# A hybrid decoder block on one core: gate tables, rank sums, and the order of two stages

## The chip, the cores and the metric

The kernel runs on one core of one Trainium2 chip. The metric is the time of one execution on the device in microseconds (us); lower is better. Engines are named as in the profile: PE is TensorE (PEld its weight loads), DVE is VectorE, ACT is ScalarE, POOL is GpSimd, and SP is SyncE, which only issues transfers.

## The reference

One decoder block over 1024 tokens of width 1024. Two mixers run in parallel on one projected input, an RWKV-7 recurrence and an attention that keeps 256 keys per query by an indexer. Sigmoid gates merge them, an output projection and a layer norm follow. Then comes a PEER mixer, the part that matters here. For each token and each of 8 heads a query is scored against two sets of 128 sub-keys; the 16 best of each set give 256 sums, the 16 best sums pick 16 experts out of 128 x 128 with softmax gates:

```
s1, i1 = top_k(s[:, :, 0], 16);  s2, i2 = top_k(s[:, :, 1], 16)
top_s, pos = top_k(s1[..., :, None] + s2[..., None, :], 16)      # flattened to 256
experts = i1[pos // 16] * 128 + i2[pos % 16];  gates = softmax(top_s)
act = gelu(h @ u[experts]) * gates;  y = sum(act * v[experts])
```

A second residual and layer norm close the block. All data are float32.

## The kernel before

The sequence is handled in two halves of 512 tokens (H = 0, 1) up to the end of the first norm. A planner lays out each engine's instructions ahead of the run, by its own model of times and by the order in which the program issues them; on the chip each engine keeps the order it was given. Several program parts are generators, and `next(side)` issues one step of another part in between.

**Merge** (`merge`, L1006). For a half, eight projections of the recurrence's output (first loop, L1016), eight of the merged rows (second loop, L1034; L1044 makes the residual sums), the norm, then eight query projections for the PEER mixer (L1092). In the second half the side work is the retrieval of token tiles 1 and 2 (a tile is 128 tokens). A step is issued in each turn of the first two loops.

**Retrieval** (`retrieve`, L1117). Six steps a tile: four of scores (a load of queries on SyncE's queue, eight matmuls against the keys, VectorE's top 16 with positions), one that merges candidates, one that turns positions into expert numbers. That last one needs sums of 16 ranks: `weighted` (L1187) multiplies 64 x 16 values in bf16 and adds them in four halvings (L1192 to L1196). It runs six times a tile.

**Two ways for the experts.** Tiles 0 to 2 gather their experts' rows one by one (`peer_gather`, L1344): GpSimd issues an indirect transfer of 128 rows (L1371), VectorE multiplies and adds (L1375 for u, L1379 for v). These gathers are spread over all of the second half of the kernel. Tiles 3 to 7 (640 tokens, `DN`) compute all 16384 experts densely and weigh them by a table of gates.

**Gate tables** (`gate_table`, L1241). For each token of tiles 3 to 7, TensorE multiplies a one-hot matrix of the second keys (128 slots x 128 keys) with one of the first keys scaled by the gates. In blocks of 8 tokens, VectorE compares the second keys (L1247, 128x1024), makes six of the eight first-key matrices (L1252) with the gate in the same instruction, and ScalarE the other two (L1254, L1255). Four tokens share a PSUM bank `tp`; a token's 128 results stand next to each other, and ScalarE's copy into `st` (L1262) reorders them, so that a key's tokens are neighbours. `st` goes to DRAM as `gtD`. Retrieval of tiles 3 to 7 and their tables run together; meanwhile TensorE computes the dots of 69 of the 128 key rows ahead of time (`dots_u`, L1630), six matmuls in each of eight steps k, from `h2T` (two halves, high and low part of the split, loaded on GpSimd's queue, L1603).

**Dense part** (L1635). 16 groups of 8 key rows. `dense_u` makes a row's activations: dots on TensorE and the gelu (L1313), or for a row ahead a load and the gelu (L1310); then the gates (L1315, from a buffer `gt` that holds four rows' gates, two buffers) and the split into two halves (L1317). `dense_v` multiplies the group before with eight column blocks of v, a block in eight steps, one per row; L1331 adds into `yacc`. Two blocks follow each of the first four rows. From the second group on, the first row that is not ahead is moved to the front (`lead`). Rows and blocks take turns in three pairs of PSUM banks (`pair`).

Of the kernel before, what the change touches and what calls it, by code (L numbers as in the profile page):

```python
# [8 lines left out]
F32 = mybir.dt.float32  # L9
# [22 lines left out]
ONE_HOT = 6  # L32
# [14 lines left out]
QS = 1  # L47
# [156 lines left out]
def body(tc, a, out, dbg=None, ntiles=8, mark=lambda s: None):  # L204
# [138 lines left out]
    ident, iota, iotan = (base.tile([128, 128], F32, name=n) for n in ("ident", "iota", "iotan"))  # L343
# [13 lines left out]
    def constants():  # L357
# [15 lines left out]
        V.tensor_scalar(iotan, iota, -1.0, None, op0=OP.mult)  # L373
# [632 lines left out]
    def merge(H, y, bz, mp, side, ties):  # L1006
# [9 lines left out]
        for d in range(8):  # L1016
# [14 lines left out]
            if H or d % QS == QS - 1:  # L1031
                next(side, None)
        vt = mp.tile([128, 8, 512], F32, name="vt")
        for d in range(8):  # L1034
# [12 lines left out]
            next(side, None)  # L1047
# [44 lines left out]
        for h in range(8):  # L1092
            w = split_w(a["wq"][h], 1024)
            pt = pacc()
            proj(pt, w, (h2T[:, 0], h2T[:, 1]), 8)
            qt = stg.tile([128, 512], F32, name="zs")
            copy(qt, pt)
            nc.sync.dma_start(qTD[H][:, h, :], qt)
        for d in range(8 if c0 < 512 else 0):
# [17 lines left out]
    def retrieve(i, keysT, tp_, then):  # L1117
# [69 lines left out]
        def weighted(ge, wt, dst):  # L1187
# [4 lines left out]
            V.tensor_tensor(pr[:, :, 0:8], pr[:, :, 0:8], pr[:, :, 8:16], op=OP.add)  # L1192
            s4 = tp_.tile([128, 64, 8], F32, name="wx")
            V.tensor_tensor(s4[:, :, 0:4], pr[:, :, 0:4], pr[:, :, 4:8], op=OP.add)
            V.tensor_tensor(s4[:, :, 0:2], s4[:, :, 0:2], s4[:, :, 2:4], op=OP.add)
            V.tensor_tensor(dst, s4[:, :, 0], s4[:, :, 1], op=OP.add)  # L1196
# [3 lines left out]
        start = tp_.tile([128, 128], BF, name="start")  # L1200
# [30 lines left out]
    def by_slot(found, dst):  # L1231
# [3 lines left out]
        for n, src in enumerate((i1, i2, gates)):  # L1235
            nc.tensor.transpose(tp[:, n * 128:(n + 1) * 128], src, ident)
        copy(dst[:, 0, :], tp[:, 0:128], scale=-1.0)
        copy(dst[:, 1:3, :].rearrange("p a b -> p (a b)"), tp[:, 128:384])


    def gate_table(i, slots, sl, du, st):  # L1241
        ng = sl.tile([128, 128], F32, name="ng")
        V.tensor_scalar(ng, slots[:, 2, :], -1.0, None, op0=OP.mult)
        for b in range(max(0, TD - i * 128) // 8, 16):
            s_ = st[:, b // 4 % 2]
            oh = du.tile([128, 16, 128], F32, name="gt", bufs=2)
            V.tensor_tensor(oh[:, 0:8], iota[:, None, :].to_broadcast([128, 8, 128]),  # L1247
                            slots[:, 1, b * 8:b * 8 + 8, None].to_broadcast([128, 8, 128]), op=OP.is_equal)
            for t in range(8):
                c = slice(b * 8 + t, b * 8 + t + 1)  # L1250
                if t < ONE_HOT:
# [443 lines left out]
```

## Time and profile before

| | us |
|---|---|
| median of 3 runs | 3887.53 (3887.27 to 4839.4) |
| profiled execution | 3874.22 |
| its span, first to last instruction | 3872.5 |
| PE busy | 3549.4 (92%) |
| DVE busy | 2759.5 (71%) |
| ACT busy | 1611.5 (42%) |
| POOL busy | 1992.2 (51%) |
| mean granted clock | 0.955 |

Busy times are unions of an engine's instructions over the whole span. They average over stages with different limits, so the rows below go by stretches, given in us from the first instruction. The granted clock is a share of TensorE's full speed.

### The profile page before, as it was taken

The page shows a single profiled execution, that of the slowest core. Times are in us where ns is not written, and L with a number is a line of the kernel's source. Part 1 is how long each engine was busy: PE and PEld are TensorE (multiplying, and loading weights), DVE is VectorE, ACT ScalarE, POOL GpSimd, SP SyncE. Part 2 cuts the span into 40 slices and gives each one's busy share as a digit, 9 for nine tenths or more (in the row PEclk, how much of TensorE's full clock was granted, in tenths as well). Part 3 has the DMA queues.
Part 4 walks back from the last instruction along what each step waited for, and adds up shares of the span by engine and source line. Part 5 has one row for each costly group of instructions (what it writes and reads, how often), then busy time and mean ns, then how long its engine had stood idle before and what let it go on. Part 6 is the DMA issues. An engine that isn't in the chain of part 4 may idle for free.

```text
span 3872.5 us, 65040 instructions
## 1 busy us (share of the span) xinstructions
PE 3549.4 (92%) x24044; PEld 3172.0 (82%) x24045; DVE 2759.5 (71%) x5983; ACT 1611.5 (42%) x2909; POOL 1992.2 (51%) x1566
## 2 busy tenths in 40 slices
PE   8989999888999998779999898899999999999997
PEld 7667776665777776669889898899999999999997
DVE  7856644857377767779999999566676666676654
ACT  3558852343444443426455463622222232222222
POOL 5442222355455543254545454266676676776655
PEclk9999998999999999889999999999999999999998
DMA  7453334765676765477777777688898988998973
GB/s 231 148 151 103 103 98 143 280 188 183 192 222 219 218 220 170 140 258 261 243 259 252 258 273 248 234 301 314 310 332 317 330 313 323 335 323 318 322 266 115
DMA packets 434994, 920.97 MB, mean 238 GB/s; under 512 B 36356, under 2 KB 195412, under 8 KB 431732
## 3 DMA queue, kind: packets, MB, share of 16 engines
q1 hardware_dynamic: 311956, 498.38, 38.5%
q0 software_dynamic: 122720, 418.43, 31.0%
q8 instruction: 190, 3.11, 0.3%
q14 instruction: 128, 1.05, 0.1%
HBM read 791.59 MB, written 125.08 MB: 237 GB/s over the span
## 4 chain that ended last, share of the span: by engine, by line
PE 33%; DVE 21%; DMA 19%; issue 10%; POOL 9%; ACT 4%; SPq 1%; POOLq 0%; ACTq 0%; DVEq 0%
DMA g<-in_v_dram,gidx 4%; PE acc L425 4%; PE acc L426 4%; PE acc L427 4%; DMA g<-in_u_dram,gidx 4%; POOL g L1371 4%; POOL wlo L1272 4%; DVE pg L1379 3%; DMA raw<-in_vt_dram 3%; DMA gt<-gtD 3%; DVE gt L1252 3%; PE pair L1285 2%; PE pair L1287 2%; PE pair L1289 2%; DMA raw<-in_ut_dram 2%
## 5 line engine op out<-in xcount | busy, mean ns | idle before, releaser
L1272 POOL TENSOR_TENSOR wlo<-raw,whi 128x1024 fp32r<-128x1024 f32 x264 | 641.0, 2429 | 285.8 <-ACT whi L233 273.6
L415 POOL TENSOR_TENSOR wlo<-wraw,whi 128x512 fp32r<-128x512 f32 x280 | 372.5, 1333 | 564.0 <-ACT whi L233 496.7
L1371 POOL DMA_INDIRECT g<-in_u_dram,gidx x384 | 403.8, 1052 | 374.0 <-DVE g L1375 211.5
L1371 POOL DMA_INDIRECT g<-in_v_dram,gidx x384 | 388.0, 1011 | 378.3 <-DVE pg L1379 192.2
L1379 DVE SCALAR_TENSOR_TENSOR pg<-g,dots,pg 128x1024 f32<-128x1024 f32 x381 | 489.3, 1284 | 120.3 <-DMA g<-in_v_dram,gidx 113.9
L1285 PE MATMUL pair<-A,whi 128*128 128x320 f32 (+2 forms) x2048 | 483.0, 312 | 38.7 <-DVE A L1317 25.9
L1285 PE MATMUL pair<-h2T,whi 128*128 128x320 f32 x2048 | 479.1, 314 | 17.3 <-DMA h2T<-h2TD 10.0
L1287 PE MATMUL pair<-h2T,whi 128*128 128x320 f32 x2048 | 482.1, 315 | 3.7 <-DMA h2T<-h2TD 3.7
L233 ACT ACTIVATE whi<-raw 128x1024 fp32r<-128x1024 f32 x264 | 278.4, 1056 | 496.2 <-PE pair L1287 194.6
L1287 PE MATMUL pair<-A,whi 128*128 128x320 f32 (+2 forms) x2048 | 480.8, 311 | 0.0
L1289 PE MATMUL pair<-A,wlo 128*128 128x320 f32 (+2 forms) x2048 | 480.2, 311 | 0.5 <-POOL wlo L1272 0.5
L1289 PE MATMUL pair<-h2T,wlo 128*128 128x320 f32 x2048 | 480.4, 314 | 0.0
L1375 DVE SCALAR_TENSOR_TENSOR g<-g,pg 128x1024 f32<-128x1024 f32 x256 | 308.3, 1216 | 106.8 <-DMA g<-in_u_dram,gidx 104.6
L1285 PEld LDWEIGHTS pair<-A,whi 128*128 128x128 f32 x2048 | 348.8, 190 | 43.3 <-issue 29.6
L425 PE MATMUL acc<-big,whi 128*128 128x512 f32 x864 | 356.3, 413 | 23.5 <-DVE zs L533 7.1
L1285 PEld LDWEIGHTS pair<-h2T,whi 128*128 128x128 f32 x2048 | 348.3, 191 | 20.2 <-issue 11.0
L1287 PEld LDWEIGHTS pair<-h2T,whi 128*128 128x128 f32 x2048 | 349.5, 191 | 5.5 <-DMA h2T<-h2TD 4.0
L427 PE MATMUL acc<-big,wlo 128*128 128x512 f32 x864 | 350.7, 406 | 2.4 <-POOL wlo L415 2.4
L426 PE MATMUL acc<-big,whi 128*128 128x512 f32 x864 | 348.9, 404 | 3.6 <-DVE big L451 3.6
L1289 PEld LDWEIGHTS pair<-h2T,wlo 128*128 128x128 f32 x2048 | 348.8, 191 | 1.5
L1289 PEld LDWEIGHTS pair<-A,wlo 128*128 128x128 f32 x2048 | 348.8, 190 | 1.0 <-POOL wlo L1272 1.0
L1287 PEld LDWEIGHTS pair<-A,whi 128*128 128x128 f32 x2048 | 349.2, 190 | 0.0
(482 smaller groups left out, 6650.4 us busy)
## 6 DMA issues: line engine op xcount, KB each, us to landing
raw<-in_vt_dram SPq DMA_DIRECT2D x136, 512.0 KB
raw<-in_ut_dram SPq DMA_DIRECT2D x128, 512.0 KB
gtD<-st SPq DMA_DIRECT2D x20, 2048.0 KB
gt<-gtD SPq DMA_DIRECT2D x32, 1280.0 KB
wraw<-in_wz_dram SPq DMA_DIRECT2D x152, 256.0 KB
dotD<-ds SPq DMA_DIRECT2D x69, 320.0 KB
al<-dotD SPq DMA_DIRECT2D x69, 320.0 KB
mw<-in_wada_dram SPq DMA_DIRECT2D x32, 512.0 KB
```

The costliest lines, as they stand in the source:

```text
L233: copy = lambda o, i, **k: A.activation(o, i, AF.Copy, **k)
L415: G.tensor_tensor(lo, raw, hi.bitcast(F32), op=OP.subtract)
L425: mm(pt, lhsT=wh[:, ks], rhs=ah[:, k, :], start=k == 0, stop=False)
L426: mm(pt, lhsT=wh[:, ks], rhs=al[:, k, :], start=False, stop=False)
L427: ins = mm(pt, lhsT=wl[:, ks], rhs=ah[:, k, :], start=False, stop=k == nk - 1)
L1272: G.tensor_tensor(lo, raw, hi.bitcast(F32), op=OP.subtract)
L1285: mm(pts[n], lhsT=wh, rhs=ah[:, h], start=k == 0, stop=False)
L1287: mm(pts[n], lhsT=wh, rhs=al[:, h], start=False, stop=False)
L1289: mm(pts[n], lhsT=wl, rhs=ah[:, h], start=False, stop=last)
L1371: G.indirect_dma_start(out=u, out_offset=None, in_=a["u" if n < 2 else "v"], in_offset=bass.IndirectOffsetOnAxis(ap=idx[:, k:k + 1], axis=0))
L1375: V.scalar_tensor_tensor(u, u, 1.0, h2, op0=OP.mult, op1=OP.mult, accum_out=dots[:, k:k + 1])
L1379: V.scalar_tensor_tensor(acc, u, dots[:, k:k + 1], acc, op0=OP.mult, op1=OP.add)
```

## The change

- **Tables.** The order of the three slot rows is changed: second keys, gates, then the first keys as bf16. For each block VectorE makes the one-hot rows of the first keys of all eight tokens in one bf16 comparison, with the token as the innermost index (`hot`). ScalarE scales each token's 128 values by the gates into float32, reading every eighth element. The matmuls write a token's results to every fourth element of the bank, and the copy into `st` no longer reorders. `iotan`, the negated gates and ScalarE's two functions go.
- **Rank sums.** One `tensor_reduce` in place of four additions; `start` becomes float32.
- **Retrieval over the second merge.** In the second half a step is issued in every second turn of the first two loops and in every second turn of the query projections.
- **Dense part.** `h2T` is loaded in eight pieces by k, both parts in each. From the second group on the rows of a group are taken in plain order, so those ahead come first.

```diff
--- before.py
+++ after.py
@@ -29,7 +29,6 @@
 AB = 12
 LAG = 4
 EARLY = 128
-ONE_HOT = 6
 M1 = 3
 J0 = 4
 JF = 0
@@ -44,7 +43,6 @@
 XOB = 2
 QIB = 2
 GM = 1
-QS = 1
 TIES = 3
 ROW0 = 8
 ROW1 = 128
@@ -340,7 +338,7 @@
         at, n = RW[name]
         nc.sync.dma_start(dst, a["rows"][0:1, at:at + n].to_broadcast([parts, n]))
 
-    ident, iota, iotan = (base.tile([128, 128], F32, name=n) for n in ("ident", "iota", "iotan"))
+    ident, iota = (base.tile([128, 128], F32, name=n) for n in ("ident", "iota"))
     ranks = base.tile([128, 3, 16], BF, name="ranks")
     eps_ln = base.tile([128, 1], F32, name="eps_ln")
     omu = cst.tile([128, 14], F32, name="omu")
@@ -370,7 +368,6 @@
         nc.sync.dma_start(pre[:, 0:128], a["more"][:, 0:128])
         V.tensor_copy(pre_b[:, 0:128], pre[:, 0:128])
         nc.sync.dma_start(iota, a["more"][:, 1152:1280])
-        V.tensor_scalar(iotan, iota, -1.0, None, op0=OP.mult)
 
         rowb(gnx.rearrange("p a b -> p (a b)"), "gng", 8)
         V.tensor_tensor(gnx, gnx, spread(), op=OP.mult)
@@ -1028,7 +1025,7 @@
             split_act(mg[:, 0, d, :], mg[:, 1, d, :], gt)
             if "merged" in dbg:
                 nc.sync.dma_start(dbg["merged"][d * 128:(d + 1) * 128, t0:t0 + 512], gt)
-            if H or d % QS == QS - 1:
+            if H == 0 or d % 2:
                 next(side, None)
         vt = mp.tile([128, 8, 512], F32, name="vt")
         for d in range(8):
@@ -1044,7 +1041,8 @@
             ins = V.scalar_tensor_tensor(vt[:, d, :], pt, modc[:, 16 + d:17 + d], xt, op0=OP.mult, op1=OP.add)
             if H:
                 anchors[2].append(ins)
-            next(side, None)
+            if H == 0 or d % 2:
+                next(side, None)
 
         h2T = big("Q")
         hl = bz.tile([128, 16, 512], F32, name="big")
@@ -1096,6 +1094,8 @@
             qt = stg.tile([128, 512], F32, name="zs")
             copy(qt, pt)
             nc.sync.dma_start(qTD[H][:, h, :], qt)
+            if H and h % 2 == 0:
+                next(side, None)
         for d in range(8 if c0 < 512 else 0):
             xa = stg.tile([128, 512], F32, name="xt")
             A.activation(xa[:, c0:], hl[:, d, c0:], AF.Identity, scale=aln[:, d:d + 1], bias=aln[:, 8 + d:9 + d])
@@ -1189,15 +1189,11 @@
             pr = wide("wp")
             V.tensor_tensor(pr.rearrange("p (a b) c -> p a b c", a=4), ge.rearrange("p (a b) c -> p a b c", a=4), wt,
                             op=OP.mult)
-            V.tensor_tensor(pr[:, :, 0:8], pr[:, :, 0:8], pr[:, :, 8:16], op=OP.add)
-            s4 = tp_.tile([128, 64, 8], F32, name="wx")
-            V.tensor_tensor(s4[:, :, 0:4], pr[:, :, 0:4], pr[:, :, 4:8], op=OP.add)
-            V.tensor_tensor(s4[:, :, 0:2], s4[:, :, 0:2], s4[:, :, 2:4], op=OP.add)
-            V.tensor_tensor(dst, s4[:, :, 0], s4[:, :, 1], op=OP.add)
+            V.tensor_reduce(dst, pr, axis=AX.X, op=OP.add)
 
         i1 = tp_.tile([128, 128], F32, name="i1")
         i2 = tp_.tile([128, 128], F32, name="i2")
-        start = tp_.tile([128, 128], BF, name="start")
+        start = tp_.tile([128, 128], F32, name="start")
         for u in range(2):
             sl = slice(64 * u, 64 * u + 64)
             first, second = (df[:, 8 * u + n:8 * u + 8:2, None, :].to_broadcast([128, 4, 16, 16]) for n in range(2))
@@ -1232,33 +1228,35 @@
 
         i1, i2, gates = found
         tp = ptp()
-        for n, src in enumerate((i1, i2, gates)):
+        for n, src in enumerate((i2, gates, i1)):
             nc.tensor.transpose(tp[:, n * 128:(n + 1) * 128], src, ident)
-        copy(dst[:, 0, :], tp[:, 0:128], scale=-1.0)
-        copy(dst[:, 1:3, :].rearrange("p a b -> p (a b)"), tp[:, 128:384])
-
-
-    def gate_table(i, slots, sl, du, st):
-        ng = sl.tile([128, 128], F32, name="ng")
-        V.tensor_scalar(ng, slots[:, 2, :], -1.0, None, op0=OP.mult)
-        for b in range(max(0, TD - i * 128) // 8, 16):
+        copy(dst[:, 0:2, :].rearrange("p a b -> p (a b)"), tp[:, 0:256])
+        copy(first_keys(dst), tp[:, 256:384])
+
+    first_keys = lambda slots: slots[:, 2, 0:64].bitcast(BF)
+
+
+    def gate_table(i, slots, sl, du, st, keys8):
+
+
+        k1 = first_keys(slots)
+        for b in range(16):
             s_ = st[:, b // 4 % 2]
-            oh = du.tile([128, 16, 128], F32, name="gt", bufs=2)
-            V.tensor_tensor(oh[:, 0:8], iota[:, None, :].to_broadcast([128, 8, 128]),
-                            slots[:, 1, b * 8:b * 8 + 8, None].to_broadcast([128, 8, 128]), op=OP.is_equal)
+            room = du.tile([128, 20, 128], F32, name="gt", bufs=2)
+            oh2, oh1 = room[:, 0:8], room[:, 8:16]
+            hot = room[:, 16:20].rearrange("p a b -> p (a b)").bitcast(BF).rearrange("p (a b) -> p a b", b=8)
+            V.tensor_tensor(hot, keys8, k1[:, None, b * 8:b * 8 + 8].to_broadcast([128, 128, 8]), op=OP.is_equal)
+            V.tensor_tensor(oh2, iota[:, None, :].to_broadcast([128, 8, 128]),
+                            slots[:, 0, b * 8:b * 8 + 8, None].to_broadcast([128, 8, 128]), op=OP.is_equal)
             for t in range(8):
-                c = slice(b * 8 + t, b * 8 + t + 1)
-                if t < ONE_HOT:
-                    V.tensor_scalar(oh[:, 8 + t], iotan, slots[:, 0, c], slots[:, 2, c], op0=OP.is_equal, op1=OP.mult)
-                else:
-                    A.activation(oh[:, 8 + t], iota, AF.Square, bias=slots[:, 0, c])
-                    A.activation(oh[:, 8 + t], oh[:, 8 + t], AF.Relu, scale=ng[:, c], bias=slots[:, 2, c])
+                copy(oh1[:, t], hot[:, :, t], scale=slots[:, 1, b * 8 + t:b * 8 + t + 1])
             for u in range(2):
-                tp = ptp()
+
+                tp = ptp().rearrange("p (a b) -> p a b", b=4)
                 for t in range(4):
-                    mm(tp[:, t * 128:(t + 1) * 128], lhsT=oh[:, 4 * u + t], rhs=oh[:, 8 + 4 * u + t], start=True, stop=True)
+                    mm(tp[:, :, t], lhsT=oh2[:, 4 * u + t], rhs=oh1[:, 4 * u + t], start=True, stop=True)
                 t0 = b % 4 * 8 + 4 * u
-                copy(s_[:, :, t0:t0 + 4].rearrange("p a b -> p b a"), tp.rearrange("p (b a) -> p b a", b=4))
+                copy(s_[:, :, t0:t0 + 4], tp)
             if b % 4 == 3:
                 nc.sync.dma_start(gtD[(i * 128 - TD) // 32 + b // 4], s_)
             yield
@@ -1599,19 +1597,21 @@
     with tc.tile_pool(reuse_waits=REUSE, name="du", bufs=1) as du, \
             tc.tile_pool(reuse_waits=REUSE, name="pg", bufs=1, space=PSUM) as pg:
         h2T = du.tile([128, 2, 8, DN], F32R, name="h2T")
-        for n in range(2):
-            G.dma_start(h2T[:, n], h2TD[:, n])
+        for k in range(8):
+            G.dma_start(h2T[:, :, k], h2TD[:, :, k])
         act = {}
         mark("retr1")
         with tc.tile_pool(reuse_waits=REUSE, name="slots", bufs=1) as sl, \
                 tc.tile_pool(reuse_waits=REUSE, name="ps2", bufs=2, space=PSUM) as banks[0]:
             st = sl.tile([128, 2, 128, 32], F32, name="st")
+            keys8 = sl.tile([128, 128, 8], BF, name="keys8")
+            copy(keys8, iota[:, :, None].to_broadcast([128, 128, 8]))
             found = {}
 
             def table(i, f=None):
                 if f:
                     by_slots(i, f)
-                found[i] = gate_table(i, slots[i], sl, du, st)
+                found[i] = gate_table(i, slots[i], sl, du, st, keys8)
 
             for i in slots:
                 table(i)
@@ -1648,11 +1648,6 @@
                 if g == 0:
 
                     first = sorted(first, key=lambda i1: (i1 in ahead, i1))
-                else:
-
-
-                    lead = next(i1 for i1 in first if i1 not in ahead)
-                    first = [lead] + [i1 for i1 in first if i1 != lead]
                 for j, i1 in enumerate(first):
                     if i1 // 4 not in gts:
                         gate_rows(i1)
```

## Rows read from the trace of the kernel before

**Rows 1.** Stretches: start:end, length; PE, PEld, DVE, ACT, POOL busy us (count); clock, DMA, GB/s
```profile
1470.00:1600.00 130.00, 104.60 (x446) 79.72 (x445) 113.27 (x519) 46.43 (x80) 40.02 (x30) 0.89 0.43 137
1600.00:1680.00 80.00, 57.94 (x245) 45.03 (x244) 35.97 (x144) 35.44 (x61) 26.70 (x21) 0.82 0.60 204
1690.00:2415.00 725.00, 654.99 (x4462) 637.43 (x4461) 709.47 (x1754) 361.92 (x596) 364.13 (x238) 0.95 0.76 258
2415.00:2475.00 60.00, 41.47 (x289) 38.54 (x290) 47.23 (x115) 50.13 (x94) 3.25 (x1) 0.91 0.36 151
2475.00:3815.00 1340.00, 1302.40 (x8755) 1296.34 (x8755) 885.56 (x1086) 372.03 (x455) 890.17 (x655) 0.99 0.87 311
```

**Rows 2.** TensorE's waits, 1690 to 2475: total us, times, longest
```profile
PE tp L1259 <- DVE gt L1252: 40.0, 21, 4.7
PE tp L1236 <- DVE i L1196: 32.5, 8, 7.7
PE tp L1259 <- ACT st L233: 12.8, 13, 1.0
```

**Rows 3.** VectorE's lines, 1690 to 2475: busy us, mean ns, idle before
```profile
L1252 DVE TENSOR_SCALAR gt<-iotan,slots 128x128 f32<-128x128 f32 x480 | 190.6, 472 | 0.0
L1379 DVE SCALAR_TENSOR_TENSOR pg<-g,dots,pg 128x1024 f32<-128x1024 f32 x127 | 162.7, 1281 | 6.8 <-DMA g<-in_v_dram,gidx 6.1 <-DVE wp L1190 0.2
...
L1194 DVE TENSOR_TENSOR wx<-wp 128x256 f32<-128x256 bf16 x30 | 30.1, 1002 | 0.7
L1192 DVE TENSOR_TENSOR wp<-wp 128x512 bf16<-128x512 bf16 x30 | 25.2, 839 | 0.4
L1195 DVE TENSOR_TENSOR wx<-wx 128x128 f32<-128x128 f32 x30 | 23.7, 790 | 0.7
...
L1184 DVE TENSOR_TENSOR ge<-wx,ranks 128x1024 bf16<-128x1024 bf16 x20 | 13.8, 692 | 0.5
...
L1196 DVE TENSOR_TENSOR i<-wx 128x64 f32<-128x64 f32 x20 | 13.7, 683 | 0.2
```

**Rows 4.** ScalarE's lines in the same stretch
```profile
L233 ACT ACTIVATE st<-tp 128x512 f32<-128x512 f32 x160 | 165.5, 1110 | 118.9 <-PE tp L1259 118.4
...
L1255 ACT ACTIVATE gt<-gt,slots,ng 128x128 f32<-128x128 f32 x160 | 70.4, 489 | 8.0 <-DVE ng L1243 7.7 <-ACT ds L233 0.3
L1254 ACT ACTIVATE gt<-iota,slots 128x128 f32<-128x128 f32 x160 | 52.6, 386 | 0.0
```

**Rows 5.** Timeline of the tail: start us, us, engine, line, operation, [idle before]
```profile
2430.43 2.07 PE L1259 MATMUL tp<-gt 128*128 128x128 f32 x16 [0.98 <-ACT st L233]
...
2431.05 1.63 DVE L1252 TENSOR_SCALAR gt<-iotan,slots 128x128 f32<-128x128 f32 x6
...
2431.09 0.65 ACT L1254 ACTIVATE gt<-iota,slots 128x128 f32<-128x128 f32 x2
...
2433.48 2.06 PE L1259 MATMUL tp<-gt 128*128 128x128 f32 x16 [0.98 <-ACT st L233]
```

**Rows 6.** TensorE's waits, 1470 to 1690
```profile
PE pair L1285 <- DMA h2T<-h2TD: 10.0, 1, 10.0
...
PE rw L1063 <- DVE vt L1044: 6.0, 2, 5.5
```

**Rows 7.** Waits from 2475 us to the end
```profile
DVE pair L1315 <- DMA gt<-gtD: 85.1, 16, 18.2
...
PE pair L1285 <- DVE A L1317: 29.5, 16, 6.6
```

**Rows 8.** Timeline at the change of groups at 3024 us
```profile
3024.00 0.46 PE L1285 MATMUL pair<-A,whi 128*128 128x320 f32 x2
...
3024.88 0.46 PE L1285 MATMUL pair<-A,whi 128*128 128x320 f32 x2
...
3027.32 0.70 ACT L1313 ACTIVATE pair<-pair 128x640 f32<-128x640 f32 x1
...
3032.82 0.82 DVE L1317 TENSOR_TENSOR A<-pair,A 128x640 fp32r<-128x640 f32 x1 [0.77 <-ACT A L233]
```

## The prediction

> **What bounds the kernel now.** I read the table of stretches first, then who waited for whom on TensorE in each stretch, then the costliest lines of the engines it waits for, and a stretch of the timeline where the waits repeat. The table cuts the part that the change touches into five [rows 1]: two for the second merge (130 and 80 us), the retrieval with its gate tables (725 us), a tail of tables (60 us) and the dense part (1340 us). The reader is to see two regimes. In the dense part TensorE is busy 1302 of 1340 us at a clock of 0.99: nothing but its own waits, 38 us, can be won. In the retrieval stretch TensorE is busy 655 of 725 us at 0.95, while VectorE is busy 709: VectorE sets the pace. TensorE's work there and in the tail at full clock is 655 x 0.95 + 41 x 0.91 = 660 us of 785, so 125 us is the most that these two can give. The waits name the cause [rows 2]: 40.0 us for VectorE's one-hot rows (L1252), 32.5 us for the expert numbers at the end of a retrieval (L1196), 12.8 us for ScalarE's evacuation of a table.
>
> The sum is made against the profiled execution, 3874.2 us (span 3872.5, 1.7 around it). The median of the runs shown is 3887.5; the difference is carried over to that median.
>
> **Tables: VectorE.** 480 one-hot instructions go; they took 190.6 us with a mean of 472 ns [rows 3]. In their place stand 80 comparisons of 128x1024 bf16 with a broadcast operand, the form of L1184, 692 ns: 55 us. That frees 135 us by the means. Where nothing disturbs them, six of the old ones take 1.63 us [rows 5], which leaves 80 x (1.63 - 0.69) = 75 us. The large f32 comparison stays, and the five negations of the gates (L1243) and one of iota go, a small gain that I leave out.
>
> **Rank sums.** In this stretch 30 trees of four additions go; the four lines took 30.1 + 25.2 + 23.7 + 13.7 = 93 us [rows 3]. 30 reductions of 128x1024 come. No row shows one of that size; the bounds are a bf16 pass over 1024 elements (L1184, 0.69 us) and an f32 pass (L1379, 1.28 us). I take 1.28, because the result is f32: 38 us, so 55 us are freed; the lower end of the gain is nothing, since the means of 0.7 to 1.0 us for such short additions hold waits that another instruction may meet instead. [...] For VectorE together: between 75 and 190 us freed, I take 130. Its load falls from 757 to 627 of 785 us.
>
> **Tables: ScalarE.** Per block of 8 tokens it now runs two Square, two Relu and two evacuations: 52.6 + 70.4 + 165.5 us over 80 blocks, 3.6 us each [rows 4]. Afterwards it runs eight scaled copies of 128x128 and two evacuations. A copy is bounded by 0.33 us (two Square in 0.65 back to back, or the mean of 0.386) and 0.49 (the Relu, which has a scale per partition like the copy). An evacuation now writes runs of four floats where it wrote single ones 128 bytes apart; its bounds are half of 1110 ns and all of it. A block costs between 3.8 and 6.1 us; I take 8 x 0.39 + 2 x 0.7 = 4.5, the scattered write being what the old price is nearest to explaining. That is 0.9 x 80 = 72 us more on an engine busy 362 of 725: hidden, as long as TensorE has other matmuls to run. If that cover is gone, as in the tail, a block's period goes from 3.05 us (2430.43 to 2433.48, where TensorE already waits 0.98 for the evacuation) [rows 5] to some 4.5, or 16 x 1.45 = 23 us.
>
> **Tables: TensorE.** The same 1280 matmul records, now writing every fourth float of a bank. They run 16 in 2.07 us, 0.13 us for 128 columns, about 1.0 ns a column [rows 5]; the dense matmuls, six of 320 columns in 0.88 us [rows 8], write a column in 0.46 ns. So the tables write at under half the rate that the port is seen to take, and I put the step at nothing; the other end is a doubling, which is a rival below.
>
> **What VectorE's time is worth.** VectorE no longer sets the pace on average, but instructions were laid out before the run and small delays still meet TensorE. I let half of the 72.5 us of waits for VectorE go, 36 us; half of the clock loss (785 - 660 less the 88 us of idle leaves 37), 18 us; and half of the 12.8 us in the tail, 6 us, because matmuls of the dots are then left to fill it. Sum -60, ends 0 and -110.
>
> **Second merge.** Of twelve retrieval steps four move out of the first two projection loops, back to the query projections. Each takes along a load on SyncE's queue, eight score matmuls, two ScalarE copies and some twenty VectorE instructions (the last two steps the merge of candidates and the rank sums, with the stores of indices and gates). They go from a stretch with VectorE busy 113 of 130 us into one with 36 of 80 [rows 1]. TensorE waited 6.0 us there for the residual sums (L1044) in one group of several [rows 6]. I take -10; ends +5 (tile 3's retrieval finds VectorE later) and -25. Queued behind the moved steps are the weight loads of the query projections and the query stores; each step holds that queue for one short issue.
>
> **Loading h2T by k.** The first dots wait 10.0 us for whole halves to land [rows 6]. Now the first of eight pieces is enough. I take -6, between 0 and -10; the six further issues delay the first gather on GpSimd's queue, on which no engine of the path waits.
>
> **Plain order.** With the leading tile gone, each of 15 groups goes from its last tile's dots straight into the projections of that group. Two things change. First, the gate rows: the leading tile asked for the second half first, so the next tile's rows had to wait for a buffer that the group before had just used. VectorE waited 85.1 us for them, and through the pair of banks held meanwhile TensorE waited 29.5 us for L1317 [rows 7]. That goes: -30. Second, the last tile's own chain (gelu, gates, two halves) loses the 7 us of the leading tile's matmuls. In the group at 3024 us TensorE ended its dots at 3024.00, the gelu started at 3027.32, and the last half was written at 3032.82 + 0.82 = 3033.64: 9.6 us, behind gathers on VectorE [rows 8]. A projection needs that tile in its eighth step, 7 x 0.88 = 6.2 us in. That is 3.4 us short in such a group; I take two thirds of it, 2.3 us, in each of 15 groups, +35. Net +5, ends -30 and +55.
>
> Sum: -60 - 10 - 6 + 5 = -71, so 3803 for the profiled execution and **3816 us** for the median.
>
> **Rivals.** *The plain order is free and VectorE's release nearly complete.* For it: without a queue blocked by late gate rows, the splits and gelus come earlier. Against: the chain above is 9.6 us with only gathers in its way. Then -90 - 15 - 6 - 25 = -136: 3752.
>
> *The freed time is refilled.* Gathers are laid into whatever VectorE leaves; 127 of them at 1281 ns ran in the stretch and waited only 6.1 us for data [rows 3], so more stand ready. 100 more would take the 130 us back, and with ScalarE's extra 72 us the tables come no sooner; the edits then do not do what they say. -10 - 6 + 15 = about 3886.
>
> *The strided bank write decides, and the kernel is slower.* The mechanism is one: a table matmul that writes every fourth float takes twice as long. 1280 x 0.13 = 166 us more on TensorE make 826 us of work where 785 stood; with some 45 us of waits left, +86, and the merge, the loads and the dense part add -10 - 6 + 15: 3973. It decides against the change from about 0.24 us a record, half as much leaves it near even. For it: no row has such a write; against it: the column rate above. [...]
>
> **How the numbers follow.** The forecast has 0.46, with a range of its own of 3780 to 3855; the first rival 0.24, the second 0.20, the third 0.10. Two per cent, about what a measurement of this kernel can tell from no change, is 78 us: 3810 and 3965. Faster: the first rival and the lower part of the forecast, 0.24 + 0.18 = 0.42. Slower: most of the third, 0.08. Within: 0.50. The range 3745 to 3900 leaves out the third rival and the far half of the first's lower side.
>
> **What would show it.** Right: L1252's successor at 0.7 us, VectorE under 90% between the merge and the dense part, that stretch some 50 to 70 us shorter, waits for gate rows in the dense part near zero, and a new wait of 2 to 4 us for L1317's successor in each first projection. Wrong: table matmul records above 0.2 us; ScalarE's copies above 0.5 us with TensorE waiting on them; gathers in the stretch up by a hundred; a dense part that is shorter by 25 us or longer by 40.

## The result, and the profile after

The changed kernel takes 3825.28 us in the median of its runs, the kernel before 3889.49 us beside it: a ratio of 0.9829 [0.9806, 0.9853]. One run of each kernel took far longer (4460.66 and 4839.4 us, the first at a granted clock of 0.70), and the ratio leaves both out. Run again beside the kernel before later, it came to 0.9855 [0.9829, 0.9881]. The profiled execution takes 3816.71 us against 3874.22, 57.5 us less. By stages, each cut at the same instruction in both traces:

| stage | before, us | after, us | difference | forecast |
|---|---|---|---|---|
| start to the second merge's first matmul | 1483.9 | 1481.1 | -2.8 | 0 |
| second merge, to the end of its last projection | 181.0 | 169.9 | -11.1 | -10 |
| from there to the first dots (with the wait for h2T) | 14.9 | 10.2 | -4.7 | -6 |
| retrieval and tables, first dots to last table | 789.3 | 767.8 | -21.5 | -60 |
| - of it behind the last projection worked ahead (tail) | 55.1 | 44.4 | -10.7 | -6 |
| dense part to the end | 1403.4 | 1386.0 | -17.4 | +5 |

The sum was near the forecast, its parts were not. The table of stretches of the changed kernel (start:end, length; PE, PEld, DVE, ACT, POOL busy us with counts; clock, DMA share, GB/s) answers to [rows 1]:

```profile
1470.00:1580.00 110.00, 96.53 (x419) 74.58 (x418) 86.79 (x341) 40.54 (x70) 38.79 (x29) 0.92 0.47 147
1580.00:1661.00 81.00, 61.42 (x260) 47.59 (x258) 57.84 (x245) 40.93 (x71) 24.70 (x23) 0.82 0.56 181
1661.00:2385.00 724.00, 668.29 (x4583) 648.83 (x4583) 601.08 (x1451) 454.69 (x916) 359.71 (x244) 0.96 0.78 270
2385.00:2429.00 44.00, 26.96 (x160) 24.74 (x160) 15.98 (x18) 41.84 (x96) 2.36 (x1) 0.82 0.30 121
2429.00:3815.00 1386.00, 1337.72 (x9016) 1334.23 (x9016) 910.74 (x1130) 388.34 (x477) 922.81 (x672) 0.98 0.85 306
```

In the third line VectorE has fallen from 98% to 83%, as forecast, but TensorE has hardly gained. In the fourth, the tail, ScalarE is busy 41.84 of 44 us. TensorE's waits from 1661 to 2429 us show the change of hands, against [rows 2]:

```profile
PE tp L1257 <- ACT st L231: 43.5, 23, 5.4
PE tp L1232 <- DVE i L1192: 9.3, 5, 3.4
```

The waits for VectorE's rows are gone and those for the expert numbers fell from 32.5 to 9.3 us; the wait for ScalarE's evacuation (st) grew from 12.8 to 43.5. Only 17.4 us of it lie in the tail; the other 26.1 stand before it, where TensorE has dots on its queue. VectorE's and ScalarE's lines there (count, busy us, mean ns, idle before), against [rows 3, 4]:

```profile
L1249 DVE TENSOR_TENSOR gt<-iota,slots 128x1024 f32<-128x1024 f32 x80 | 99.5, 1244 | 1.1 <-ACT slots L231 1.1
L1248 DVE TENSOR_TENSOR gt<-keys,slots 128x1024 bf16<-128x1024 bf16 x80 | 80.9, 1016 | 43.3 <-issue 36.2 <-PE tp L1257 7.0
...
L1192 DVE TENSOR_REDUCE i<-wp 128x64 f32<-128x1024 bf16 x20 | 24.4, 1218 | 0.6
```

```profile
L231 ACT ACTIVATE gt<-gt,slots 128x128 f32<-128x128 bf16 x640 | 274.5, 526 | 91.0 <-DVE gt L1248 83.1 <-DVE v L1140 4.4 <-issue 2.5
L231 ACT ACTIVATE st<-tp 128x512 f32<-128x512 f32 x159 | 87.4, 594 | 41.0 <-PE tp L1257 37.9 <-issue 3.1
```

ScalarE's block is (274.5 + 88.0) / 80 = 4.5 us (88.0 with the 160th evacuation, which ends just past the window), the value taken. The tail's timeline (start us, us, engine, line, what, idle before) answers to [rows 5]:

```profile
2408.06 1.13 ACT L231 ACTIVATE st<-tp 128x512 f32<-128x512 f32 x2
2408.76 2.88 PEld L1257 LDWEIGHTS tp<-gt 128*128 128x128 f32 x16 [2.40 <-ACT st L231]
2408.76 3.17 PE L1257 MATMUL tp<-gt 128*128 128x128 f32 x16 [2.21 <-ACT st L231]
2409.01 3.48 ACT L231 ACTIVATE gt<-gt,slots 128x128 f32<-128x128 bf16 x8
...
2412.30 1.14 ACT L231 ACTIVATE st<-tp 128x512 f32<-128x512 f32 x2
```

ScalarE runs without a gap: two evacuations, eight copies for the block after, two evacuations, 4.26 us a block (3.05 before). TensorE, with nothing else on its queue, stands behind the copies. In the dense part VectorE's waits for gate rows fell from 85.1 us to one of 22.1 [rows 7], and TensorE's wait for A is 24.0 us in eight waits instead of 29.5 in sixteen:

```profile
DVE pair L1313 <- DMA gt<-gtD: 22.1, 1, 22.1
```

```profile
PE pair L1283 <- DVE A L1315: 24.0, 8, 5.3
```

### The profile page after: what moved, and what is told of

Read it like the earlier page. It is cut to its first block, busy times and chain, and to the rows that moved or that the text cites. A ratio compares the mean times of both kernels' runs of the same rounds, so it can differ in the third digit from the quotient of the medians.

```text
span 3814.9 us, 64785 instructions
## 1 busy us (share of the span) xinstructions
PE 3540.3 (93%) x24045; PEld 3168.1 (83%) x24045; DVE 2604.9 (68%) x5433; ACT 1695.8 (44%) x3230; POOL 1981.9 (52%) x1572
## 4 chain that ended last, share of the span: by engine, by line
PE 33%; DMA 13%; DVE 12%; POOL 7%; issue 6%; ACT 4%; POOLq 0%; DVEq 0%; SPq 0%; ACTq 0%
PE pair L1283 7%; PE pair L1285 7%; PE pair L1287 7%; DMA g<-in_v_dram,gidx 5%; DMA g<-in_u_dram,gidx 4%; POOL g L1369 3%; POOL wlo L1270 3%; DVE pg L1377 2%; PE acc L422 2%; DMA raw<-in_ut_dram 2%; PE acc L424 2%; PE acc L423 2%; ACT gt L231 2%; DVE g L1373 2%; DMA raw<-in_vt_dram 2%
## 5 line engine op out<-in xcount | busy, mean ns | idle before, releaser
L1369 POOL DMA_INDIRECT g<-in_v_dram,gidx x384 | 376.1, 979 | 288.2 <-DVE pg L1377 138.9
```

Of the source, the lines that this page charges most:

```text
L1369: G.indirect_dma_start(out=u, out_offset=None, in_=a["u" if n < 2 else "v"], in_offset=bass.IndirectOffsetOnAxis(ap=idx[:, k:k + 1], axis=0))
```

## The experiments

Ratios are to the kernel before, with 95% intervals; the change itself stands at 0.9829 and 0.9855. "Behind" is the number of table blocks (of 80) that stand on TensorE's queue after the last projection worked ahead, counted in each trace: 16 before, 10 in the changed kernel. Ratios come from several runs, stretches and waits from the one profiled execution, which lies up to 13 us from the median of its kernel's runs, in undo_sums 26 above it. The edits are shown shortened. First the change was taken apart.

**undo_tables**

```diff
-copy(oh1[:, t], hot[:, :, t], scale=gate)            # and the strided bank write
+V.tensor_scalar(oh, iotan, key, gate, is_equal, mult) # t < 6; else two ScalarE instructions
```

> The changed kernel, but its gate tables are built as before (f32 one-hot rows, six first-key rows by VectorE and two by ScalarE pairs, the reordering evacuation); rank sums by one instruction, merge spacing, h2T by k and plain order stay. From the first dots to the last table the kernel before took 789 us, the changed one 768. Theory A (ScalarE now sets the pace of the tables, so the table edit alone is worth little and the rank sums bring the rest): the stretch comes to 765 to 778 us, the whole within 10 us of the changed kernel (3825 to 3835), TensorE's waits for VectorE's one-hot rows are back at 30 to 40 us and those for ScalarE's evacuation fall from 43 to about 13 us. Theory B (the tables bring all of the 21 us, the sums none): the stretch is back at 785 to 795 us, the whole at 3840 to 3850.

Measured: 0.9770 [0.9743, 0.9796], below both intervals of the change. Stretch 744.7 us (735.2 + tail 9.5), 2 behind. The waits moved as theory A said (42.0 us for VectorE's rows, 3.1 for evacuations), but neither theory expected this size: by the two ratios of the change, **its new tables cost it 23 to 33 us.**

```profile
1662.00:2397.00 735.00, 683.67 (x4709) 664.88 (x4710) 713.02 (x1832) 407.82 (x685) 360.14 (x237) 0.96 0.77 265
2397.00:2407.00 10.00, 6.39 (x36) 5.59 (x34) 10.00 (x19) 5.36 (x8) 4.53 (x3) 0.83 0.76 258
```

```profile
PE tp L1257 <- DVE gt L1250: 42.0, 27, 3.1
```

VectorE is busy 97% here and TensorE waits 42 us for it, and yet the whole is shorter: these are 27 short waits in a stretch that holds 8 blocks more. Of the 23.1 us between the stretches, TensorE's idle time makes 18.0 (72.6 against 54.6), 13.9 of that in the tails (17.4 against 3.5).

**undo_sums**

```diff
-V.tensor_reduce(dst, pr, axis=AX.X, op=OP.add)
+# the three halving additions and the last, as before
```

> The changed kernel with the four additions of the rank sums restored, all else as changed. Theory A (the sums bring most of what the retrieval won: TensorE's wait for the expert numbers was 32.5 us before and is 9.3 us after): first dots to last table goes from 768 to 780 to 790 us, the wait for the expert numbers to 25 us or more, the whole to 3837 to 3847. Theory B (tables bring it): stretch within 5 us of 768, the whole at 3820 to 3830.

Measured: 0.9914 [0.9894, 0.9933]. Theory A by the whole and by the wait for the expert numbers, which is back; the stretch of 796.0 us, with a tail of 81.6 and 16 behind, is above its range, in a profiled execution 26 us over the median:

```profile
PE tp L1236 <- DVE i L1196: 37.6, 5, 10.2
```

The second merge also starts later, at 1499.0 us; in the other kernels it starts between 1474 and 1492.

**undo_order**

```diff
+else:
+    lead = next(i1 for i1 in first if i1 not in ahead)
+    first = [lead] + [i1 for i1 in first if i1 != lead]
```

> The changed kernel with the not-ahead tile of each group computed first in the dense part, as before. Theory A (the plain order itself is what the dense part won): the dense part goes from 1386 back to 1400 to 1405 us, the whole to 3840, VectorE's waits for gate rows in the dense part are back at 80 us, and sixteen short waits of TensorE for A, some 29 us, take the place of eight, 24 us. Theory B (the dense part's 17 us came from elsewhere, such as the state in which the retrieval leaves the gathers and the load queue): dense part within 5 us of 1386, the whole at 3820 to 3830.

Measured: 0.9886 [0.9867, 0.9905], above the first interval of the change, overlapping the second. Theory A in the dense part: 1400.7 us against 1386.0 (1390.7 in the unedited kernel's second profile, so the order is worth 10 to 15 us), and VectorE's waits for gate rows are back. TensorE's waits for A hardly differ: 26.6 us in twelve, against 24.0 (25.9 in the second profile). What TensorE waits for more is the addition into `yacc`. Its retrieval was 9 us longer with the same tables and sums; the unedited kernel's two profiles differ by 6 us there, so I read nothing from it.

```profile
DVE pair L1313 <- DMA gt<-gtD: 87.9, 16, 22.4
```

```profile
PE pair L1283 <- DVE A L1315: 26.6, 12, 5.1
PE pair L1283 <- DVE yacc L1329: 7.1, 2, 5.4
```

**undo_merge**

```diff
-if H == 0 or d % 2:
-    next(side, None)
+next(side, None)        # in both projection loops; none in the query projections
```

> The changed kernel with the retrieval steps spaced as before in the second merge (every turn of both projection loops, none in the query projections). Theory A (the spacing wins some 11 us in the merge, and keeps them): the first dots start at 1670 to 1676 us instead of 1661, the retrieval stretch stays at 768, the whole at 3835 to 3840. Theory B (the steps only move; what the merge wins the retrieval gives back): first dots at 1670 to 1676, the retrieval stretch 755 to 760 us, the whole within 5 us of 3825.

Measured: 0.9846 [0.9825, 0.9867], theory B. From the merge's first matmul to the first dots, and from there to the last table, undone and then as changed:

```profile
1479.00:1669.00 190.00, 148.86 (x629) 114.20 (x628) 133.91 (x591) 79.70 (x135) 59.41 (x49) 0.88 0.48 151
1669.00:2428.00 759.00, 692.16 (x4743) 668.50 (x4743) 615.47 (x1458) 499.04 (x1013) 368.98 (x244) 0.97 0.76 264
```

```profile
1481.00:1661.00 180.00, 146.95 (x629) 113.81 (x628) 142.35 (x582) 79.41 (x136) 58.92 (x48) 0.87 0.50 157
1661.00:2429.00 768.00, 695.25 (x4743) 673.57 (x4743) 617.06 (x1468) 496.53 (x1011) 362.07 (x245) 0.96 0.75 261
```

The spacing wins 10 us in the merge, and the retrieval gives 9 of them back. The two profiles of the unedited kernel differ by 6 us in that stretch, so the 9 is rough; the whole shows no gain either.

Then the cost of the tables: is it the tail without cover, or ScalarE's load?

**extra16**

```diff
-EXTRA = 10
+EXTRA = 16
```

> The changed kernel with 75 instead of 69 first projections worked ahead during the retrieval (six more, about 7 us of TensorE each, taken out of the dense part; the sum of work is the same). With the new tables 10 of the 80 table blocks stand behind the last of the projections on TensorE's queue; here 1 does. Theory A (the new tables cost time because their last ten blocks run with nothing beside them, at ScalarE's 4.26 us a block, 44 us for 20 us of matmuls): the stretch from first dots to last table grows from 768 to 785 to 790 us although it holds 43 us more work, the dense part shrinks from 1386 to 1343, the whole is 18 to 25 us under the changed kernel, a ratio of 0.977 to 0.978. Theory B (ScalarE's and VectorE's load in the whole stretch sets the time, the tail is only where it shows): the tables end as much later as there is more work, the whole within 5 us of the changed kernel, ratio 0.982 to 0.984.

Measured: 0.9795 [0.9782, 0.9808], below the second interval of the change and just touching the first. Theory A, though the ratio gains less than it said: stretch 781.6 us, dense part 1344.8, together 27 us less than in the changed kernel. The wait for the evacuation fell from 43.5 us, though not away:

```profile
PE tp L1257 <- ACT st L231: 24.4, 14, 6.0
```

**split6**

```diff
+if t >= 6: V.tensor_scalar(oh1[:, t], hot[:, :, t], gate, None, op0=OP.mult)
+else: copy(oh1[:, t], hot[:, :, t], scale=gate)
```

> The changed kernel, but two of the eight gate copies of a block are made by VectorE (a multiplication by the gate) instead of ScalarE: ScalarE's block falls from 4.5 to some 3.6 us, VectorE's grows by some 0.6 us; 7 blocks instead of 10 stand behind the last projection worked ahead. Theory A (ScalarE in the tail is what costs): a block of the tail takes 3.4 to 3.8 us instead of 4.26, the tail 25 to 28 us instead of 44, TensorE's wait for ScalarE's evacuation 20 to 25 us instead of 43.5, the whole 15 to 22 us under the changed kernel, ratio 0.977 to 0.979. Theory B (VectorE, 83% busy, still sets the pace of the stretch): its 50 us more come back as waits, the whole is the same or up to 10 us longer, ratio 0.983 to 0.986.

Measured: 0.9805 [0.9789, 0.9821]. Tail 24.5 us for 7 blocks, 3.5 us each, as theory A said; VectorE's 64 us of new copies did not come back as waits of that size. The ratio lies between the two theories' ranges, and its interval overlaps the first of the change's two, so the whole is told apart less well than the tail.

```profile
2399.00:2424.00 25.00, 15.85 (x114) 14.25 (x112) 16.00 (x24) 23.83 (x54) 2.84 (x1) 0.93 0.40 162
```

```profile
PE tp L1261 <- ACT st L231: 25.6, 22, 2.9
...
PE tp L1261 <- DVE gt L1254: 10.7, 8, 1.9
```

**split6_extra13** (both edits, with EXTRA = 13)

> Both edits at once: two of eight gate copies on VectorE, and three more first projections worked ahead (72), which leaves 1 block behind the last of them. Theory A (only the uncovered tail costs): no more than the better of the two alone, ratio 0.975 to 0.978, and with the tail gone TensorE waits for ScalarE's evacuation under 10 us. Theory B (the engines' load in the stretch costs beside the tail): VectorE's 50 us more show as waits for the one-hot rows above 20 us and the ratio stays at 0.980 to 0.983.

Measured: 0.9753 [0.974, 0.9766], the lowest ratio of all, with no tail left: theory A's ratio, but not its claim that only the tail costs, since the wait for evacuations was still 16.2 us; that for one-hot rows was 12.2. It is below both intervals of the change, and not told apart from undo_tables.

**bank_only** (undo_tables, with the strided bank write kept)

```diff
+tp = ptp().rearrange("p (a b) -> p a b", b=4)
+mm(tp[:, :, t], lhsT=..., rhs=...);  copy(s_[:, :, t0:t0 + 4], tp)
```

> The kernel with the tables of before (which, with the rest of the change, ran at a ratio of 0.977) and only one part of the new tables: the matmuls write their banks strided, and the evacuation copies in 16-byte runs instead of 4-byte pieces. Theory A (the write costs nothing and the cheaper evacuation takes some 80 us off ScalarE, which nothing waited for more than 3 us): ScalarE's evacuation falls from 1.11 to about 0.6 us, table matmuls stay at 0.29 us, the whole within 5 us of 0.977. Theory B (ScalarE's evacuations hold the banks and so TensorE, in the tail above all): 8 to 15 us shorter, ratio 0.973 to 0.975. Theory C (the strided write does cost): table matmuls above 0.35 us, the whole 10 us or more longer, ratio 0.980 and up.

Measured: 0.9798 [0.9785, 0.9812]. The durations are theory A's: the evacuation nearly halves (1.11 us in [rows 4]), and the table matmuls do not change (292 ns before, 294 in the changed kernel). Nothing becomes faster; in undo_tables TensorE waited only 3.1 us for evacuations. The whole is 11 us over 0.977, outside theory A's 5 us, but the two intervals overlap and the unedited kernel itself came out 10 us apart in its two series, so the whole neither shows nor excludes a cost of that size.

```profile
L232 ACT ACTIVATE st<-tp 128x512 f32<-128x512 f32 x160 | 95.0, 597 | 168.3 <-PE tp L1257 167.8
```

```profile
L1257 PE MATMUL tp<-gt 128*128 128x128 f32 x1280 | 178.0, 292 | 45.1 <-DVE gt L1250 42.2 <-ACT st L232 1.6 <-ACT whi L232 1.0
```

**bank5_extra13** (bank_only with ONE_HOT = 5 and EXTRA = 13)

> Tables of before with the strided bank write, but five first-key rows of a block by VectorE and three by ScalarE pairs (instead of six and two), and three more projections worked ahead (72). ScalarE's two evacuations of a block are 1.05 us shorter by the write and a pair costs it 0.88 us, so its block stays at 3.5 us; VectorE gets 80 rows of 0.41 us, 33 us, less than in the same kernel with six. Theory A (with the tail covered, VectorE's pace in the stretch is what is left): TensorE's wait for the one-hot rows falls from 42 us to 20 to 30, ratio 0.972 to 0.976. Theory B (what is left is not VectorE's, the waits move on to ScalarE): waits for ScalarE's pairs or evacuations take their place, ratio 0.977 to 0.981.

Measured: 0.9789 [0.9763, 0.9814]; the ratio is theory B's, but neither theory's waits came. They neither fell nor moved to ScalarE:

```profile
PE tp L1257 <- DVE gt L1250: 44.9, 19, 7.2
PE tp L1234 <- DVE i L1194: 15.5, 5, 4.9
```

Theory A's premise came only in part: the 400 rows left take VectorE 180.3 us where 480 took 195.3 in bank_only, 15 us less and not 33. What holds the waits is open; VectorE is busy 711 of 770 us.

**tables_only** (the kernel before with the new tables alone)

> The kernel before with the new tables alone: old rank sums, old spacing, old dense order, h2T by halves. In it 16 blocks stand behind the last projection worked ahead, as in the kernel before. Theory A (the tables cost 23 us wherever they stand): ratio 1.004 to 1.008, with a tail of 16 blocks of 4.26 us instead of 3.05, 68 us for 49. Theory B (the cost depends on what else bounds the stretch; beside the slow rank sums VectorE sets the pace, and what the tables take off it pays for the slower tail): ratio 0.996 to 1.000, the stretch from first dots to last table within 8 us of before's 789, its tail 65 to 85 us and its first part that much shorter. Worked out from the runs: slow sums and new tables with all other parts ran at 0.9914, and plain order is worth some 0.006 of that. Theory C (the tables' 75 to 135 us of VectorE count as predicted): 0.985 to 0.990.

Measured: 1.0043 [1.0022, 1.0065], theory A at its lower end. Stretch 803.7 us. Before, cut at the start of its tail, and below it tables_only:

```profile
1680.00:2414.00 734.00, 661.27 (x4487) 643.09 (x4487) 716.16 (x1805) 363.75 (x599) 365.13 (x239) 0.95 0.76 260
2414.00:2469.00 55.00, 36.58 (x256) 33.71 (x256) 47.88 (x117) 49.02 (x93) 3.25 (x1) 0.91 0.32 132
```

```profile
1677.00:2412.00 735.00, 662.92 (x4486) 647.64 (x4487) 605.17 (x1496) 430.94 (x859) 354.66 (x239) 0.93 0.75 260
2412.00:2481.00 69.00, 41.90 (x259) 38.28 (x257) 25.59 (x28) 66.41 (x154) 2.36 (x1) 0.80 0.25 104
```

111 us less of VectorE made the first part no shorter; all of the loss, 14 us, is in the tail, where 16 blocks take 4.3 us each on a busy ScalarE. In the first part TensorE's waits changed hands. Before, and below it tables_only:

```profile
PE tp L1259 <- DVE gt L1252: 34.3, 19, 4.4
```

```profile
PE tp L1259 <- ACT st L232: 13.0, 6, 5.4
...
PE tp L1125 <- ACT st L232: 8.9, 5, 5.2
```

With 4.1 us for the dots' copies and 3.4 for the scores', ScalarE's share is 29.4 us there, where it was 2.0.

**after_again** (the changed kernel, unedited)

> The changed kernel as it is, beside the kernel before, so that the others of this call and the earlier ratios have it on one scale. Theory A (the tables' uncovered tail is worth about 20 us: six more projections ahead, 0.9795, and two copies moved to VectorE, 0.9805, both removed it): the ratio is 0.982 to 0.985. Theory B (those two gained nothing that can be told from the scatter between calls): 0.979 to 0.981.

Measured: 0.9855 [0.9829, 0.9881], just above theory A's range. The two series of this kernel lie 0.0026 apart; split6_extra13 is 0.0076 below the lower, more than such scatter, extra16 0.0034, which its trace (27 us less by stages) has to support.

**hot32**

```diff
-keys8 = sl.tile([128, 128, 8], BF);   first_keys = slots[:, 2, 0:64].bitcast(BF)
+keys8 = sl.tile([128, 128, 8], F32);  first_keys = slots[:, 2, :]
```

> The changed kernel with its first-key comparison reading f32 operands (still writing bf16). One look, for the durations of that one instruction: with bf16 operands 80 of it take 0.68 us each undisturbed but 1.016 in the mean, since ten take 2.3 to 3.3 us, and those ten begin while a GpSimd tensor instruction of the weight split is under way. Theory A (only the faster mode of the bf16 comparison is held up by GpSimd): all 80 take 1.2 to 1.3 us, none above 1.5, as the f32 comparison beside it does (1.244 in the mean). Theory B (any VectorE instruction there is held up, by a transfer or by the operands' place): some still take 2.3 us and more, the mean is above 1.45 us. Its whole time is not read: VectorE has up to 20 us more, and 16 instead of 10 blocks stand behind the last projection worked ahead.

Measured: theory A fell and theory B's figures came, twelve of the 80 take 2.4 to 4.0 us and the mean is 1.56:

```profile
L1248 DVE TENSOR_TENSOR gt<-keys,slots 128x1024 bf16<-128x1024 f32 x80 | 124.7, 1564 | 34.0 <-issue 20.6 <-ACT gt L231 8.7 <-PE tp L1257 4.7
```

The causes that theory B names (a transfer, the operands' place) are not needed: the held instructions go with the weight split, as the last section shows. Not all of them begin while a split is under way, as the expectation has it: in the changed kernel eight of twelve begin 0.3 to 0.5 us before the split's record.

## Why the prediction was right or wrong

**Right in size** (3816 us forecast, 3825 measured; within 2% of before, the likeliest case), but only by luck: two wrong terms had errors of opposite signs, -60 where -21.5 came, +5 where -17.4 came.

**Right steps.** The rank sums take VectorE 24.4 + 12.1 = 36.5 us (38 forecast; the 93 us that they replace leave out the ten sums into `start`, 3.1 us). ScalarE's block is 4.5 us, the value taken, though from dearer copies (0.43 us where 0.39 was taken) and cheaper evacuations (0.55 where 0.7 was). The strided bank costs nothing that the records show, so rival 3 fell: 1280 matmul records of 294 ns against 292, and one starts every 112 ns (median) in both. The doubling that it was worked out from was an estimate, and no run shows it. The sign "above 0.2 us" for this write was misplaced, since a record is longer than the step from one to the next and stood at 292 ns before the change. The wait for h2T before the first dots fell from 10.0 to 4.4 us, for 6 forecast. Rival 2's refill by gathers did not come: 127 and 44 gathers' arithmetic in the stretch, as before.

**The step that failed: "hidden as long as TensorE has other matmuls".** ScalarE's 72 us more were put at nothing where other matmuls stand, and the tail, whose price was named (a period of 4.5 us instead of 3.05), went into the sum as -6. Neither held. TensorE's waits for VectorE's rows and expert numbers fell from 72.5 to 9.3 us, by more than the 36 of the sum; its waits for ScalarE's evacuations grew from 12.8 to 51.0, 43.5 ahead of tables and 7.5 ahead of the scores, which use the same two banks `tp`. Most of them stand in the first part, under the cover that was to hide them:

```profile
PE tp L1257 <- ACT st L231: 26.1, 13, 5.4
...
PE tp L1127 <- ACT st L231: 7.5, 3, 5.2
```

That part won 10.7 us where some 54 of the 60 were forecast. In the tail ten blocks run with no other matmul, at 4.26 us; with the old tables only two do (undo_tables). That the table of stages has -10.7 there is the work of six blocks fewer behind, not of the tables. The new tables alone lose 14 us of stretch: in the tail nothing hides ScalarE, in the first part its waits take the place of VectorE's (tables_only). Giving the tail cover (extra16) wins back 13 to 23 us by the two ratios, two copies off ScalarE (split6) 9 to 19. Of the signs of being wrong that the prediction gave, "ScalarE's copies above 0.5 us with TensorE waiting on them" came: 526 ns in the mean.

**"The value of VectorE's time" went with it.** I valued the 130 us that I took as freed at -60, by their share in the waits, for tables and sums alike. VectorE's time was not worth the same everywhere. The sums sit in a chain, from a retrieval's end to the blocks that need it. With them shorter, tables stand earlier on TensorE's queue (16 behind to 10 with new tables, by undo_sums; 16 to 2 with old, from the kernel before to undo_tables, where the other parts differ too), and undoing them costs 0.6 to 0.9% of the time. Taking the table rows off VectorE gave the first part nothing, 735 us with VectorE at 98% or at 82%, because the work went to ScalarE and the waits with it. What they would be worth with ScalarE unchanged, no run shows.

**Second merge:** -11.1 for -10, but not a gain: undone, it comes back in the retrieval.

**Plain order:** +5 forecast, -10 to -15 in the dense part by undo_order, and neither of its two terms came. The -30 was to be TensorE's wait for A: VectorE's waits for gate rows fell from 85.1 to 22.1 us, but the wait for A only from 29.5 to 24.0. The +35, for each group's last tile in step eight of the projection, did not come either: that step waited 0.6 us in one group. The waits for A stand ahead of the projection's very first matmul, which does not read that tile's halves. In all eight the write of A that ends 0.14 to 0.15 us before that matmul is the one of the group's seventh row, counted in VectorE's order; the eighth row's ends 4 to 8 us later. With three pairs of banks in turn, the pair of the seventh row is the one that the projection takes (row eight and the next group's first row take the other two). So they are waits for a pair of banks, by the trace; no run with more pairs was made. Of undo_order's 14.7 us, some 9 are TensorE's waits (41.8 us in all against 32.6), 7.1 of these for `yacc`.

Some 6 us of the dense part's 17 lie after the last dense matmul (22.2 us before, 16.1 after), where the store's end comes sooner; they stayed in every run but tables_only and were not traced to a part. Each part but h2T by k was undone alone without losing them, and h2T was not undone alone.

**A better version** is split6_extra13. Undoing the tables alone does about as much.

## What to carry to other kernels

Before work is moved to an idle engine, find the stretch where that engine's chain runs with nothing beside it, count the items there, and multiply by the new period: that product, not the busy share, was the price here (16 blocks of 4.3 us made a tail of 69 us in tables_only, 55 before). Cover alone did not make the rest free: TensorE waited 26.1 us for ScalarE's evacuations where it had dots on its queue, so compare the waits for both engines before and after. Time taken off a busy engine counted where other work waits at the end of its chain (0.6 to 0.9% of the time for the rank sums) and not elsewhere (111 us less of VectorE in tables_only made the first part no shorter); test it by undoing each part alone, since tables and sums, which look additive, had opposite signs here. When a sum comes out right, check its terms.

## What the runs showed of the hardware

In the changed kernel 32 pairs of records of VectorE's table comparisons and GpSimd's weight split overlap between the first dots and the last table; counting back from each record's end by its kind's median, no two overlap by more than 0.17 us. By the trace the two hardly work at the same time: the records read as if one stood still until the other ended. Two of the pairs:

```profile
1801.29 1.22 DVE L1249 TENSOR_TENSOR gt<-iota,slots 128x1024 f32<-128x1024 f32 x1
1801.43 3.35 POOL L1270 TENSOR_TENSOR wlo<-raw,whi 128x1024 fp32r<-128x1024 f32 x1
...
1914.92 3.28 DVE L1248 TENSOR_TENSOR gt<-keys,slots 128x1024 bf16<-128x1024 bf16 x1
1915.25 2.39 POOL L1270 TENSOR_TENSOR wlo<-raw,whi 128x1024 fp32r<-128x1024 f32 x1
```

In the first pair GpSimd's record is 1 us over its median of 2.41; in the second VectorE's is 2.6 us over 0.69 and ends 0.56 us after GpSimd's, although its record begins first. Every first-key comparison that was held ends 0.55 to 0.56 us after the split when its operands are bf16, and 1.08 to 1.09 us after it when they are f32 (hot32), so bf16 is not what decides:

```profile
1763.42 3.74 DVE L1248 TENSOR_TENSOR gt<-keys,slots 128x1024 bf16<-128x1024 f32 x1
1763.68 2.39 POOL L1270 TENSOR_TENSOR wlo<-raw,whi 128x1024 fp32r<-128x1024 f32 x1
```

So f32 comparisons are held too, against theory A: here 3.74 us where the median of the 80 is 1.22, and in the changed kernel one comparison of the second keys takes 3.44 us, also with a median of 1.22. Why one holds up the other, no run shows. Which of the two is held does not follow from the starts of the records: in eight of the twelve held bf16 comparisons VectorE's record begins first, as in the second pair. In the retrieval, what VectorE's instructions that overlap a split run beyond the median of their kind (where that is over 15% plus 60 ns) comes to 140 us before, 61 of it in the first-key rows (26 of the 480), and to 49 us in the changed kernel, 27 of it in the bf16 comparisons (12 of the 80). The 61 us are the gap between the forecast's 135 us by means and 75 us undisturbed; the 27 us are, over the 80, the gap between the mean of the bf16 comparison, 1016 ns, and its median, 685.
